# A convolution half-chunk moved behind the first half's sums, and the last output chunk finished by 128 tokens

## The chip, the cores and the metric

The kernel runs on one core of a Trainium2 chip, all work in one launch. The metric is the device time of one execution in microseconds (us). Before the change the median of three runs is 1165.35 us (1165.35 to 1165.51).

A core has five instruction streams that meet only at semaphores: TensorE (PE, matmuls; PEld is its weight load, which runs beside them), VectorE (DVE), ScalarE (ACT), GpSimd (POOL) and SyncE (SP, which here only issues DMAs). Each stream runs its instructions in the order in which the program wrote them.

## The reference, cut to what matters

Two layers over 512 tokens of width 1024, in float32. Layer 0 mixes by gating and attention, layer 1 by a convolution module; each is followed by a squared-ReLU MLP. The two places that the change touches are the convolution of layer 1 and the last norm.

```python
def conformer_conv(h, w_pw1, b_pw1, w_dw, b_dw, ln_g, ln_b, w_pw2, b_pw2):
    a, gate = jnp.split(h @ w_pw1 + b_pw1, 2, axis=-1)
    y = a * jax.nn.sigmoid(gate)
    y = lax.conv_general_dilated(y, w_dw[:, None, :], ...)   # 31 taps along the tokens, each channel alone
    y = jax.nn.silu(layernorm(y, ln_g, ln_b))                # over the 1024 channels of a token
    return y @ w_pw2 + b_pw2
...
x = x + g2 * sq_relu_mlp(...)
return rmsnorm(x, final_g)
```

## The kernel before

**Layout.** Everything is transposed: channels lie on the 128 partitions in 8 chunks, tokens along the free axis (512, in two halves of 256, a0:a1 and b0:b1). Each float32 product is made of three matmuls from a high and a low part (`mm3`, line 87; `together`, line 214, does it for several output chunks at once). The order on every engine is the order in which the Python code is run; no scheduler moves anything (`manual_schedule`).

**The convolution module** (`conv_module`, from line 1360). `glu(c)` makes channel chunk c of the gated input, for c = 2 to 7 here (0 and 1 were made in the norm before). Chunks 1 and 2 are convolved on DVE, tap by tap, from a queue of small jobs (`aux`, `work`). Chunks 0, 3, 4, 5, 6, 7 are convolved on PE: `evac_glu` copies the padded chunk into four tiles `y4` of 32 channels at four shifts (16 copies of 32 partitions, lines 1307 to 1314), all by DMA on SP, but of chunk 7 ten by DMA and six by ACT (line 1312). `conv_steps` (line 1327) then makes 32 matmuls for a half of 256 tokens, one after another into one PSUM bank, and ACT adds the bias (line 1336) into `zc`. It is a generator that can stop between steps of k.

**The layer norm over channels** needs, for each token, the sum and the sum of squares over all 8 chunks. `take(c)` (line 1345) subtracts a base value (line 1349), squares on ACT (line 1356) and adds to the two running sums (lines 1357, 1358). When the last chunk of a half is in, `sums` (line 1418) adds over the partitions by eight tiny matmuls (line 1422) and makes mean and variance (lines 1424 to 1426), and POOL the inverse root (line 1427); `stats` n = 0 and 1 spread mean and inverse root over the partitions by two matmuls each (line 1434), and ACT copies them to `mur` (line 1436). `normed` is a generator over chunks: subtract (1444), scale (1447), SiLU (1452), split in high and low part (lines 93, 94). Its outputs `ch` are the operands of the next product, `together(four, ch, ...)`, whose first matmul therefore waits for chunk 0 of `normed`.

**The order around the change.** Written a for the first half of the tokens and b for the second, PE does 5a, 5b, 6a, 7a, 6b, `sums` of half a, a first piece of 7b, `stats` 0, a second piece, `stats` 1, the rest of 7b, then the product. `W.pieces(4)` between 5b and 6a cuts the four pieces of a weight tile in high and low parts (line 148 on ACT, line 143 on DVE) and, with the last, has the next tile loaded on SP (line 124).

**The end** (`tail1`). Output chunk 7 of half b is the last product. Before the change, DVE adds it to `x` in one instruction of 256 tokens (line 1073), ACT squares it (line 343), and PE sums the squares over the partitions by two matmuls for each 128 tokens (line 1575): one over `acc` (chunks 0 to 6), one over the last square. Then root (1577), reciprocal (1578), spread by PE (1581), copy (1583), eight multiplications (1586) and four output DMAs on SP (1588).

In the trace one matmul of float32 operands shows as two records, so a half chunk of 32 matmuls has 64.

Of the kernel before, what the change touches and what calls it, by code (L numbers as in the profile page):

```python
# [13 lines left out]
AF = mybir.ActivationFunctionType  # L14
# [3 lines left out]
P = 128  # L18
# [4 lines left out]
H = T // 2  # L23
# [32 lines left out]
def body(ctx: ExitStack, tc: tile.TileContext, I: dict, out: bass.AP):  # L56
    nc = tc.nc
    act, dve, pool, pe, sync = nc.scalar, nc.vector, nc.gpsimd, nc.tensor, nc.sync
# [19 lines left out]
    def slot(dt=F32, cols=512, s="t"):  # L78
        return bp.tile([P, cols], dt, tag="tmp", name=nm(s), bufs=6)
# [92 lines left out]
    for l in range(2):  # L172
        s = [I["w_ff1"][l, i] for i in range(4)]
        for g in range(1, 4):
# [5 lines left out]
    W = Weights([w_in[i] for i in (4, 5, 8, 9, 6, 7, 2, 3, 0, 1)] + [I["w_out"][i] for i in range(4)]  # L180
                + ff_srcs[0] + [I["w_pw1"][i] for i in range(8)] + [I["w_pw2"][i] for i in range(4)]
                + ff_srcs[1])
# [31 lines left out]
    def together(ms, acts, evac, t0=0, t1=T, ks=range(KC), hook=None):  # L214

        ks = list(ks)
        pss = [bank()[:, : t1 - t0] for _ in ms]
        for n, k in enumerate(ks):
            a = acts[k][0][:, t0:t1], acts[k][1][:, t0:t1]
            for (m, w, c), ps in zip(ms, pss):  # L220
                pe.matmul(ps, w[0][:, k, c : c + P], a[0], start=n == 0, stop=False)  # L221
                pe.matmul(ps, w[1][:, k, c : c + P], a[0], start=False, stop=False)  # L222
            for (m, w, c), ps in zip(ms, pss):
                pe.matmul(ps, w[0][:, k, c : c + P], a[1], start=False, stop=n == len(ks) - 1)  # L224
            if hook:
                hook(n)
        return [lambda m=m, ps=ps: evac(m, ps, t0, t1) for (m, w, c), ps in zip(ms, pss)]
# [31 lines left out]
    for k in range(0, KC, 2):  # L259
        t = mpa.tile([P, 2, 512], F32, tag="ablk", name=nm("x0"), bufs=6)  # L260
# [42 lines left out]
    for k in range(0, KC, 4):  # L303
        t = mpa.tile([P, 4, TC], F32, tag="ablk", name=nm("ctx"), bufs=6)
# [4 lines left out]
    ones = cp.tile([P, P], F32, name="ones")  # L309
# [108 lines left out]
    for k in range(KC):  # L418
        sq = slot(s="sq")
# [649 lines left out]
        sync.dma_start(x[:, 4 * i : 4 * i + 4, :], I["xT"][:, 4 * i : 4 * i + 4, :])  # L1069

    def residual(gate, ss):
        def evac(m, ps, t0, t1):
            dve.scalar_tensor_tensor(x[:, m, t0:t1], ps, gate[:, m : m + 1], x[:, m, t0:t1],  # L1073
                                     op0=ALU.mult, op1=ALU.add)
            if ss is not None:
                ss.add(x[:, m, t0:t1], t0, t1)
        return evac

# [248 lines left out]
    def conv_steps(c, t0, t1, stops=()):  # L1327
        wd = cv["matrices"][c]
        ps = bank()[:, : t1 - t0]
        for k in range(8):  # L1330
            if k in stops:
                yield
            for g in range(4):
                pe.matmul(ps[32 * g : 32 * g + 32, :], wd[:, g * 8 + k, :],  # L1334
                          cv["y4"][c, g][:, 4 * k + t0 : 4 * k + t1], start=k == 0, stop=k == 7)
        act.activation(zs[c][:, t0:t1], ps, AF.Identity, bias=vcol(V_BDW, c))
        yield

    def conv_pe(c, t0=0, t1=T):
        run(conv_steps(c, t0, t1))  # L1340
# [4 lines left out]
    def take(c, t0=0, t1=T):  # L1345

        lsum, lsq = cv["sums"]
        z = zs[c][:, t0:t1]
        dve.tensor_tensor(z, z, cv["m0"][:, t0:t1], op=ALU.subtract)
        if not cv["begun"]:  # L1350
            cv["begun"] = True
            dve.tensor_copy(lsum[:, t0:t1], z)
            act.activation(lsq[:, t0:t1], z, AF.Square)
        else:
            sq = slot(cols=t1 - t0, s="sq")
            act.activation(sq, z, AF.Square)
            dve.tensor_tensor(lsum[:, t0:t1], lsum[:, t0:t1], z, op=ALU.add)
            dve.tensor_tensor(lsq[:, t0:t1], lsq[:, t0:t1], sq, op=ALU.add)

    def conv_module(h):  # L1360
# [46 lines left out]
        preload(AF.Silu)  # L1407
        work(100)
        conv_pe(5, a0, a1)
        conv_pe(5, b0, b1)  # L1410
        take(5)
        W.pieces(4)
        conv_pe(6, a0, a1)
        lsum, lsq = cv["sums"]
        ch = [pair(s="ch") for _ in range(KC)]
        stat = {}

        def sums(t0, t1):
            ps = bank()[:, :4]
            for i in range(4):  # L1420
                b = t0 + i % 2 * P
                pe.matmul(ps[:, i : i + 1], (lsum, lsq)[i // 2][:, b : b + P], ones[:, :1], start=True, stop=True)  # L1422
            q = small(8, "q")
            dve.tensor_scalar(q[:, 0:4], ps, 1.0 / D, None, op0=ALU.mult)
            dve.tensor_tensor(q[:, 4:6], q[:, 0:2], q[:, 0:2], op=ALU.mult)
            dve.scalar_tensor_tensor(q[:, 4:6], q[:, 2:4], EPS, q[:, 4:6], op0=ALU.add, op1=ALU.subtract)
            pool.tensor_tensor(q[:, 2:4], q[:, 4:6], expo[:, :2], op=ALU.pow)
            stat[t0] = q, vp.tile([P, T], F32, tag="mur", name=nm("mur"), bufs=2), bank()

        def stats(t0, n):  # L1430

            q, r, ps = stat[t0]
            for i in (2 * n, 2 * n + 1):
                pe.matmul(ps[:, i * P : (i + 1) * P], q[:, i : i + 1].to_broadcast([P, P]), ident,  # L1434
                          start=True, stop=True)
            act.copy(r[:, n * H : n * H + H], ps[:, n * H : n * H + H])
# [18 lines left out]
        def go(gen, n=1):  # L1455
            for _ in range(n):
                next(gen, None)
# [2 lines left out]
        conv_pe(7, a0, a1)  # L1460
        take(7, a0, a1)
        conv_pe(6, b0, b1)
        sums(a0, a1)
        last = conv_steps(7, b0, b1, (1, 4))
        next(last)
        stats(a0, 0)
        na = normed(a0, a1)
        take(6, b0, b1)
        go(na)
        next(last)  # L1470
        stats(a0, 1)
        go(na, 2)
        next(last)
        go(na)
# [57 lines left out]
    def tail1(acts, ev, ss, ff, third):  # L1532

        (a0, a1), (b0, b1) = HALVES
        oa, ob = (wp.tile([P, KC, H], F32, tag="raw", name=nm("o"), bufs=2) for _ in range(2))

        def gained(ks, o=ob, t0=b0, t1=b1):
            for k in ks:
                act.activation(o[:, k, :], x[:, k, t0:t1], AF.Copy, scale=vcol(V_FG, k))

        def finish(ks, r):
            for k in ks:
                dve.scalar_tensor_tensor(oa[:, k, :], x[:, k, a0:a1], vcol(V_FG, k), r, op0=ALU.mult, op1=ALU.mult)  # L1543
            sync.dma_start(out[:, ks[0] : ks[-1] + 1, a0:a1], oa[:, ks[0] : ks[-1] + 1, :])

        w = W.use()
        for i in range(2):
            chunk(4 + i, w, i * P, acts, ev, 0, t0=a0, t1=a1)
        v = W.use()
        for i in range(2):  # L1550
            chunk(6 + i, v, i * P, acts, ev, 0, t0=a0, t1=a1)
            gained((2 * i, 2 * i + 1))
        gained((6, 7), oa, a0, a1)
        four = together([(4, w, 0)], acts, ev, b0, b1, hook=lambda n: ss.total(a0, a1) if n == 5 else None)[0]
        four()
        r = ss.rstd(a0, a1)
        finish((0, 1, 2), r)
        gained((4,))
        chunk(5, w, P, acts, ev, 0, t0=b0, t1=b1)
        finish((3, 4, 5), r)  # L1560
        gained((5,))
        chunk(6, v, 0, acts, ev, 0, t0=b0, t1=b1)
        for k in (6, 7):
            pool.tensor_tensor(oa[:, k, :], oa[:, k, :], r, op=ALU.mult)
        sync.dma_start(out[:, 6:8, a0:a1], oa[:, 6:8, :])
        gained((6,))
        ss.flush()
        seven = together([(7, v, P)], acts, ev, b0, b1)[0]
        seven()
        gained((7,))  # L1570
        sq, ss.late = ss.late[0], None
        tot_ = bank()
        for n in range(2):
            for i, t in enumerate((ss.acc[:, b0:b1], sq)):
                pe.matmul(tot_[:, n : n + 1], t[:, n * P : n * P + P], ones[:, :1], start=i == 0, stop=i == 1)
        q = small(2, "q")
        act.activation(q, tot_[:, :2], AF.Sqrt, bias=epsc, scale=1.0 / D)
        dve.reciprocal(q, q)
        pr = bank()[:, :H]
        for n in range(2):  # L1580
            pe.matmul(pr[:, n * P : n * P + P], q[:, n : n + 1].to_broadcast([P, P]), ident, start=True, stop=True)
        r = slot(cols=H, s="rstd")
        act.copy(r, pr)
        for e, ks in ((dve, (0, 1)), (pool, (2,)), (dve, (3, 4)), (pool, (5,)), (dve, (6, 7))):
            for k in ks:
                e.tensor_tensor(ob[:, k, :], ob[:, k, :], pr if e is dve else r, op=ALU.mult)
        for k0, k1 in ((0, 1), (1, 3), (3, 6), (6, 8)):
            sync.dma_start(out[:, k0:k1, b0:b1], ob[:, k0:k1, :])
        ff.close()

    mlp(1, lead1, 0, tail1)
# [84 lines left out]
```

## Time and profile before

| | |
|---|---|
| median of three runs | 1165.35 us |
| the profiled execution: its own time, its span | 1164.55 us, 1162.8 us |
| ACT and POOL, share of the span busy | 41%, 13% |
| DMA traffic, mean over the span | 139 GB/s |
| longest idle time of PE by the profile's list of waits | 1.0 us, at the start |

A page of the profile has times from one execution on the chip; a line of a timeline gives start, duration, engine, line of the program, operation, output and inputs, how many instructions were merged, and in brackets the idle time ahead of it with what ended it. Matmul records overlap: a record of 256 columns lasts 0.28 to 0.4 us while the next one starts 0.12 us later, so stretches are read from starts, not from durations. A stretch of merged matmuls counts as busy also where it contains a short wait.

### The profile page before, as it was taken

The page shows a single profiled execution, that of the slowest core. Times are in us where ns is not written, and L with a number is a line of the kernel's source. Part 1 is how long each engine was busy: PE and PEld are TensorE (multiplying, and loading weights), DVE is VectorE, ACT ScalarE, POOL GpSimd, SP SyncE. Part 2 cuts the span into 40 slices and gives each one's busy share as a digit, 9 for nine tenths or more (in the row PEclk, how much of TensorE's full clock was granted, in tenths as well). Part 3 has the DMA queues.
Part 4 walks back from the last instruction along what each step waited for, and adds up shares of the span by engine and source line. Part 5 has one row for each costly group of instructions (what it writes and reads, how often), then busy time and mean ns, then how long its engine had stood idle before and what let it go on. Part 6 is the DMA issues. An engine that isn't in the chain of part 4 may idle for free. (4 is left out here: it accounts for less than half of the span.)

```text
span 1162.8 us, 16541 instructions
## 1 busy us (share of the span) xinstructions
PE 1150.3 (99%) x6612; PEld 956.9 (82%) x6612; DVE 724.8 (62%) x1258; ACT 479.7 (41%) x955; POOL 153.0 (13%) x149
## 2 busy tenths in 40 slices
PE   9999999999999999999999999999999999999997
PEld 5788898889888888888889666699888888888887
DVE  4855786878665665666677879577643443443544
ACT  5564557446422422423246223575531331332423
POOL 0041234433000000000024110153100000000001
PEclk9999999999999999999999999999999999999998
DMA  9634543351565555555531444313232232232222
GB/s 370 247 125 134 167 149 110 121 192 62 205 236 181 188 210 181 191 207 181 203 123 56 145 126 125 98 37 110 73 109 100 82 109 102 79 109 78 105 73 73
DMA packets 32333, 161.91 MB, mean 139 GB/s; under 512 B 4416, under 2 KB 8000, under 8 KB 16256
## 3 DMA queue, kind: packets, MB, share of 16 engines
q1 hardware_dynamic: 28224, 146.43, 36.5%
q10 hardware_dynamic: 4032, 14.42, 3.6%
q8 instruction: 52, 0.85, 0.3%
q14 instruction: 25, 0.20, 0.1%
HBM read 152.52 MB, written 2.10 MB: 133 GB/s over the span
## 5 line engine op out<-in xcount | busy, mean ns | idle before, releaser
L148 ACT CAST whi<-raw 128x512 fp32r<-128x512 f32 x340 | 191.5, 616 | 196.4 <-PE ps L90 171.9
L88 PE MATMUL ps<-hhi,whi 128*128 128x512 f32 x608 | 238.5, 392 | 0.0
L89 PE MATMUL ps<-hhi,wlo 128*128 128x512 f32 x608 | 236.8, 389 | 0.0
L90 PE MATMUL ps<-hlo,whi 128*128 128x512 f32 x608 | 236.8, 389 | 0.0
L143 DVE TENSOR_TENSOR wlo<-raw,whi 128x512 fp32r<-128x512 f32 x293 | 200.3, 721 | 37.1 <-ACT whi L148 36.3
L90 PE MATMUL ps<-hid,whi 128*128 128x512 f32 (+1 forms) x520 | 196.5, 378 | 0.0
L89 PE MATMUL ps<-hid,wlo 128*128 128x512 f32 (+1 forms) x520 | 196.5, 378 | 0.0
L88 PE MATMUL ps<-hid,whi 128*128 128x512 f32 (+1 forms) x520 | 196.4, 378 | 0.0
L1073 DVE SCALAR_TENSOR_TENSOR x<-ps,mod,x 128x512 f32<-128x512 f32 (+1 forms) x94 | 62.7, 669 | 147.5 <-PE ps L90 142.6
L88 PEld LDWEIGHTS ps<-hhi,whi 128*128 128x128 f32 x608 | 114.2, 188 | 26.6 <-issue 3.2
L90 PEld LDWEIGHTS ps<-hlo,whi 128*128 128x128 f32 x608 | 114.1, 188 | 23.9
L89 PEld LDWEIGHTS ps<-hhi,wlo 128*128 128x128 f32 x608 | 114.2, 188 | 23.0
L143 POOL TENSOR_TENSOR wlo<-raw,whi 128x512 fp32r<-128x512 f32 x47 | 70.0, 1503 | 416.9 <-DVE mod L599 306.8
L599 DVE CUSTOM_DVE_ANT_0 graw<-graw,cB,vec 128x1024 f32<-128x1024 f32 x80 | 109.0, 1364 | 20.8 <-DMA graw<-in_wmB_dram 20.8
L89 PEld LDWEIGHTS ps<-hid,wlo 128*128 128x128 f32 x520 | 97.9, 188 | 18.2
L88 PEld LDWEIGHTS ps<-hid,whi 128*128 128x128 f32 x520 | 97.8, 188 | 18.2
L90 PEld LDWEIGHTS ps<-hid,whi 128*128 128x128 f32 x520 | 97.9, 188 | 17.9
L1209 DVE TENSOR_TENSOR z<-z 128x512 f32<-128x512 f32 (+1 forms) x72 | 46.8, 656 | 90.8 <-ACT z L1207 90.7
L1207 ACT ACTIVATE z<-ps 128x512 f32<-128x512 f32 (+1 forms) x72 | 38.9, 549 | 131.5 <-PE ps L90 129.3
L1213 DVE TENSOR_TENSOR hid<-z,hid 128x512 fp32r<-128x512 f32 (+1 forms) x72 | 45.7, 641 | 43.3 <-ACT hid L1211 43.3
L1211 ACT CAST hid<-z 128x512 fp32r<-128x512 f32 (+1 forms) x72 | 40.6, 572 | 60.6 <-DVE z L1209 60.6
L343 ACT ACTIVATE sq<-x 128x256 f32<-128x256 f32 (+1 forms) x41 | 20.3, 496 | 66.4 <-DVE x L1073 66.3
(271 smaller groups left out, 1712.3 us busy)
## 6 DMA issues: line engine op xcount, KB each, us to landing
raw<-in_w_ff_dram SPq DMA_DIRECT2D x64, 1024.0 KB
graw<-in_wmB_dram SPq DMA_DIRECT2D x28, 1024.0 KB
graw<-in_wmB_dram ACTq DMA_DIRECT2D x24, 512.0 KB
raw<-in_w_pw_dram SPq DMA_DIRECT2D x12, 1024.0 KB
raw<-in_w_in_dram SPq DMA_DIRECT2D x8, 1024.0 KB
wmA<-in_wmA_dram SPq DMA_DIRECT2D x7, 1024.0 KB
y<-ypad SPq DMA_DIRECT2D x90, 67.5 KB
raw<-in_w_out_dram SPq DMA_DIRECT2D x4, 1024.0 KB
```

The lines of the kernel that those rows point to most:

```text
L88: pe.matmul(ps, w[0], a[0], start=first, stop=False)
L89: pe.matmul(ps, w[1], a[0], start=False, stop=False)
L90: pe.matmul(ps, w[0], a[1], start=False, stop=last)
L143: (e or dve).tensor_tensor(lo.parts[q], src, hi.parts[q].bitcast(F32), op=ALU.subtract)
L148: act.copy(hi.parts[q], src)
L343: act.activation(sq, src, AF.Square)
L599: dve.tensor_tensor_reduce(out=wv, in0=wv, in1=cB, scale=1.0, scalar=vcol(V_BMOD, l * 48 + q * 8 + j % 8), op0=ALU.mult, op1=ALU.add, accu ...
L1073: dve.scalar_tensor_tensor(x[:, m, t0:t1], ps, gate[:, m : m + 1], x[:, m, t0:t1], op0=ALU.mult, op1=ALU.add)
L1207: act.activation(z, ps, AF.Relu)
L1209: dve.tensor_tensor(z, z, z, op=ALU.mult)
L1211: act.copy(hi, z)
L1213: dve.tensor_tensor(lo, z, hi.bitcast(F32), op=ALU.subtract)
```

## The change

In the convolution, chunk 5 is convolved for half a only at first. Its half b is done as `five`, behind `sums` of half a, in two pieces around `stats` 0, and 7b is done in two pieces behind `stats` 1. The four weight pieces, which stood together, are spread: behind 5a, 6a, 6b and 5b. `take(5)` is split into its halves; `take(5, b0, b1)` comes last but one. At the end, the residual add and the square of the last chunk are done for 128 tokens at a time, the two matmuls over `acc` come first, and the matmul over a square follows each square. The third of the four last output DMAs is issued by ACT.

```diff
     def residual(gate, ss):
-        def evac(m, ps, t0, t1):
+        def evac(m, ps, t0, t1, sq=None):
             dve.scalar_tensor_tensor(x[:, m, t0:t1], ps, gate[:, m : m + 1], x[:, m, t0:t1], ...)
-            if ss is not None:
+            if sq is not None:
+                act.activation(sq, x[:, m, t0:t1], AF.Square)
+            elif ss is not None:
                 ss.add(x[:, m, t0:t1], t0, t1)
...
         conv_pe(5, a0, a1)
-        conv_pe(5, b0, b1)
-        take(5)
-        W.pieces(4)
+        W.pieces(1)
+        take(5, a0, a1)
         conv_pe(6, a0, a1)
+        W.pieces(1)
...
         conv_pe(7, a0, a1)
         take(7, a0, a1)
         conv_pe(6, b0, b1)
+        W.pieces(1)
         sums(a0, a1)
-        last = conv_steps(7, b0, b1, (1, 4))
-        next(last)
+        five, last = conv_steps(5, b0, b1, (4,)), conv_steps(7, b0, b1, (4,))
+        next(five)
+        take(6, b0, b1)
         stats(a0, 0)
         na = normed(a0, a1)
-        take(6, b0, b1)
         go(na)
+        next(five)
+        W.pieces(1)
+        stats(a0, 1)
         next(last)
-        stats(a0, 1)
+        take(5, b0, b1)
         go(na, 2)
         next(last)
...
-        seven = together([(7, v, P)], acts, ev, b0, b1)[0]
-        seven()
-        gained((7,))
-        sq, ss.late = ss.late[0], None
+        last = []
+        together([(7, v, P)], acts, lambda m, ps, t0, t1: last.append(ps), b0, b1)[0]()
+        sq = slot(cols=H, s="sq")
         tot_ = bank()
         for n in range(2):
-            for i, t in enumerate((ss.acc[:, b0:b1], sq)):
-                pe.matmul(tot_[:, n : n + 1], t[:, n * P : n * P + P], ones[:, :1], start=i == 0, stop=i == 1)
+            pe.matmul(tot_[:, n : n + 1], ss.acc[:, b0 + n * P : b0 + n * P + P], ones[:, :1],
+                      start=n == 0, stop=False, skip_group_check=True)
+        for n in range(2):
+            t = slice(n * P, n * P + P)
+            ev(7, last[0][:, t], b0 + n * P, b0 + n * P + P, sq[:, t])
+            pe.matmul(tot_[:, n : n + 1], sq[:, t], ones[:, :1], start=False, stop=True, skip_group_check=True)
+        gained((7,))
...
-            sync.dma_start(out[:, k0:k1, b0:b1], ob[:, k0:k1, :])
+            (act if k0 == 3 else sync).dma_start(out[:, k0:k1, b0:b1], ob[:, k0:k1, :])
```

How the instructions stand now, at three places. First PE, where its second half-chunk of this stretch ends. The names y_923 to y_926 are the four tiles of chunk 5, y_937 to y_940 those of chunk 6, y_952 to y_955 those of chunk 7; in brackets stand the semaphores that a row waits for, those of DMAs by queue. Before:

```order
3703 L1334 MATMUL ps_6615<-y_925_6320,graw_5871 32x256
3704 L1334 MATMUL ps_6615<-y_926_6325,graw_5871 32x256
3705 L1334 MATMUL ps_6666<-y_937_6421,graw_5871 32x256 [waits DMAHW3_49,DMAHW2_49,DMAHW4_49,DMAHW1_49,Pool_49]
3706 L1334 MATMUL ps_6666<-y_938_6426,graw_5871 32x256 [waits DMAHW6_49,DMAHW7_49,DMAHW5_49,DMAHW0_49]
3707 L1334 MATMUL ps_6666<-y_939_6431,graw_5871 32x256 [waits DMAHW3_49,DMAHW4_49,DMAHW2_49,DMAHW1_49]
3708 L1334 MATMUL ps_6666<-y_940_6436,graw_5871 32x256 [waits DMAHW6_49,DMAHW7_49,DMAHW5_49,DMAHW0_49]
```

And with the change, in the same rows:

```order
3703 L1336 MATMUL ps_6624<-y_939_6431,graw_5871 32x256
3704 L1336 MATMUL ps_6624<-y_940_6436,graw_5871 32x256
3705 L1336 MATMUL ps_6681<-y_952_6559,cB 32x256 [waits DMAHW4_49,DMAHW5_49,DMAHW3_49,DMAHW2_49]
3706 L1336 MATMUL ps_6681<-y_953_6564,cB 32x256 [waits DMAHW6_49,DMAHW7_49,DMAHW1_49,DMAHW0_49]
3707 L1336 MATMUL ps_6681<-y_954_6569,cB 32x256 [waits DMAHW3_49,DMAHW2_49,Activation_49]
3708 L1336 MATMUL ps_6681<-y_955_6574,cB 32x256 [waits Activation_49]
```

Chunk 7 stood third among the half-chunks behind the last `glu` product (5a, 5b, 6a came first) and now stands one half-chunk, 32 matmuls, earlier.

Second ACT, from the bias of 6b (zc_6420) to the first operand of the product (chhi). zc_6309 is chunk 5, zc_6558 chunk 7, zc_5834 chunk 0. Before:

```order
567 L1336 ACTIVATE zc_6420<-ps_6760,vec 128x256 [waits PE_49]
568 L1436 COPY mur_6804<-ps_6805 128x256 [waits PE_49]
569 L1356 ACTIVATE sq_6815<-zc_6420 128x256 [waits DVE_49]
570 L1436 COPY mur_6804<-ps_6805 128x256 [waits DVE_49,PE_49]
571 L1452 ACTIVATE zc_5834<-zc_5834,vec 128x256 [waits DVE_49]
572 L93 CAST chhi_6700<-zc_5834 128x256 [waits Activation_49]
```

With the change:

```order
566 L1338 ACTIVATE zc_6420<-ps_6720,vec 128x256 [waits PE_49]
567 L148 CAST whi_6615<-raw_6408 128x512
568 L1358 ACTIVATE sq_6786<-zc_6420 128x256 [waits DVE_49,Activation_49]
569 L1438 COPY mur_6766<-ps_6767 128x256 [waits PE_49]
570 L1338 ACTIVATE zc_6309<-ps_6768,vec 128x256 [waits PE_49]
571 L148 CAST whi_6615<-raw_6408 128x512
572 L1438 COPY mur_6766<-ps_6767 128x256 [waits DVE_49,PE_49]
573 L1358 ACTIVATE sq_6836<-zc_6309 128x256 [waits DVE_49,Activation_49]
574 L1454 ACTIVATE zc_5834<-zc_5834,vec 128x256 [waits DVE_49]
575 L93 CAST chhi_6660<-zc_5834 128x256 [waits Activation_49]
```

Four instructions came in: two weight casts, and the bias and the square of 5b. On DVE the matching low parts (line 143) and the three instructions of `take(5, b0, b1)` came in ahead of the scaling of chunk 0 (line 1447).

Third PE at the end of the program, from the last matmul of the last product on. Before:

```order
5914 L224 MATMUL ps_9982<-hid_9535,whi_9768 128x256
5915 L1575 MATMUL ps_10011<-ones,acc_9637 128x1 [waits DVE_49]
5916 L1575 MATMUL ps_10011<-ones,sq_10008 128x1 [waits Activation_49]
5917 L1575 MATMUL ps_10011<-ones,acc_9637 128x1
5918 L1575 MATMUL ps_10011<-ones,sq_10008 128x1
```

With the change:

```order
5914 L224 MATMUL ps_9987<-hid_9540,whi_9773 128x256
5915 L1579 MATMUL ps_10013<-ones,acc_9642 128x1 [waits DVE_49]
5916 L1579 MATMUL ps_10013<-ones,acc_9642 128x1
5917 L1584 MATMUL ps_10013<-ones,sq_10012 128x1 [waits Activation_49] x2
5918 L1591 MATMUL ps_10026<-kon,q_10023 128x128 [waits DVE_49]
```

Both matmuls over `acc` now stand ahead of the first that waits for a square.

## The prediction

> **What bounds the kernel now.** The page first: the share of each engine, and the clock by slices.
>
> ```profile
> span 1162.8 us, 16541 instructions
> PE 1150.3 (99%) x6612; PEld 956.9 (82%) x6612; DVE 724.8 (62%) x1258; ACT 479.7 (41%) x955; POOL 153.0 (13%) x149
> ...
> PEclk9999999999999999999999999999999999999998
> ```
>
> PE is the bound, at its full clock to the last slice. So a change of order can only win PE's idle time or shorten the end, and loses what it adds of either. Next the timeline of PE over the convolution, to find the idle time there.
>
> ```profile
> 725.38 10.57 PE L1334 MATMUL ps<-y,graw 128*32 128x256 f32 x192
> 735.77 0.59 PE L1334 MATMUL ps<-y,cB 128*32 128x256 f32 x2
> 736.55 4.14 PE L1334 MATMUL ps<-y,cB 128*32 128x256 f32 x60 [0.19 <-issue]
> ...
> 744.29 1.05 PE L1422 MATMUL ps<-ones,lsum 128*128 128x1 f32 x8
> ...
> 745.85 0.71 PE L1434 MATMUL ps<-kon,q 128*128 128x128 f32 x4
> 746.49 1.50 PE L1334 MATMUL ps<-y,cB 128*32 128x256 f32 x24
> 748.53 0.68 PE L1434 MATMUL ps<-kon,q 128*128 128x128 f32 x4 [0.54 <-DVE zc L1444]
> 749.14 1.94 PE L1334 MATMUL ps<-y,cB 128*32 128x256 f32 x32
> 751.20 0.39 PE L221 MATMUL ps<-chhi,whi 128*128 128x256 f32 x1
> ```
>
> The reader sees 5a, 5b and 6a as one block: 192 records in 10.57 us, so 3.52 us for each half chunk and 0.055 us a record. Then 7a (the rows with cB) limps until about 737.2; then it and 6b run dense; `sums` at 744.29; 7b in pieces with 0.54 us of idle time in front of `stats` 1; the product begins at 751.20. The idle time that can be won is that 0.54 us, the limping of 7a, and a few tenths. PEld shows 7a better:
>
> ```profile
> 736.52 0.14 PEld L1334 LDWEIGHTS ps<-y,cB 128*32 128x32 f32 x2 [0.64 <-issue]
> 737.23 2.98 PEld L1334 LDWEIGHTS ps<-y,cB 128*32 128x32 f32 x58 [0.57 <-ACT zc L1336]
> ```
>
> The first tile of chunk 7 is there when PE comes, the second at 736.52, the third at 737.23. The profile names an ACT bias for the last, but the tile hangs on two DMAs and two ACT copies, so I look at SP.
>
> ```profile
> 721.56 3.12 SPq L1314 DMA_DIRECT2D y<-ypad  x5
> 726.51 0.33 SPq L124 DMA_DIRECT2D raw<-in_w_pw_dram  x1
> ...
> L1314 SPq DMA_DIRECT2D y<-ypad x10: 507/585/1799, 727.2 to 733.9; - x10
> ...
> 726.00:726.50 0.50, 0.50 (x18) 0.27 (x10) 0.50 (x2) 0.00 (x0) 0.00 (x0) 1.00 0.00 0
> ```
>
> The ten DMAs of chunk 7 are issued from 727.2 to 733.9, behind a weight load that shares the DMA engines. The five issues before them end at 724.68; one takes 0.585 us, so the last began at about 724.1, and by 726.0 the DMA engines are idle (last row, 0.00): 2.0 us from issue to landing. The last of chunk 7 began at 733.9 and should land at 735.9; PE got it at 737.23. It is **a transfer, not PE, that sets when 7a runs**.
>
> **The change part by part.** *5b out of the way of 7a.* PE now reaches 7a after two half chunks, at 725.38 + 2 x 3.52 = 732.42, and nothing in SP's order or in the weight load ahead moves. So PE waits where it used to work. Until when? At the latest 737.23, as now. At the earliest 735.9, without what delayed that last DMA by 1.3 us; it is an estimate from these rows:
>
> ```profile
> q8 instruction: 52, 0.85, 0.3%
> ...
> q8 instruction: 1, 0.02, 4.4%
> ```
>
> The first is of the whole span, the other of 733.5 to 735.5: one packet of instructions is fetched in the midst of the copies, and the issue beside it took 1.799 us. 6612 matmuls on 52 packets are 127 on one: the pace of PE's own stream. In this run it came at some 154 records behind 725.38 (8.5 us by 0.055); the new order has only 128 records ahead of 7a, so the same fetch falls behind the copies. I take 735.9, a gain of 1.33 us on the start of 7a, and keep 0 as the other end. PE's wait grows from about 1.3 us to 3.5, with one pair of records at each landed tile.
>
> *From 7a to the product.* Behind the start of 7a everything is as before up to `sums`; from there to the product it was 751.20 - 744.29 = 6.91 us. Now (clock at 0 with `sums`): 1.0 for it, first part of 5b 1.76, `stats` 0 0.7, second part 1.76: 5.25. The bias of 5b on ACT comes next, then a chain across engines:
>
> ```profile
> 744.40 0.47 ACT L1336 ACTIVATE zc<-ps,vec 128x256 f32<-128x256 f32 x1 [2.07 <-PE ps L1334]
> 734.66 2.16 ACT L148 CAST whi<-raw 128x512 fp32r<-128x512 f32 x4
> 735.39 2.49 DVE L143 TENSOR_TENSOR wlo<-raw,whi 128x512 fp32r<-128x512 f32 x4
> 745.85 0.42 DVE L1349 TENSOR_TENSOR zc<-zc,m 128x256 f32<-128x256 f32 x1
> 749.65 0.42 DVE L1447 TENSOR_TENSOR zc<-zc,ps 128x256 f32<-128x256 f32 x1 [1.27 <-ACT mur L1436]
> 750.11 0.60 ACT L1452 ACTIVATE zc<-zc,vec 128x256 f32<-128x256 f32 x1 [0.49 <-DVE zc L1447]
> 750.74 0.40 ACT L93 CAST chhi<-zc 128x256 fp32r<-128x256 f32 x1
> ```
>
> Bias of 5b from 5.6 (6b's began at 744.40, 0.11 us behind the next PE work, and that is here `stats` 1 at 5.45) to 6.1; weight cast 0.54 to 6.6; low part on DVE 0.62 to 7.3; `take(5)` three instructions of 0.42 with the square between, to 8.6; scale of chunk 0 0.42 to 9.0; SiLU and cast 1.05 with hand-overs of about 0.05, to 10.1. So the product begins at 10.1 instead of 6.91: **+3.2 us**. PE's own work comes to 9.7 (5.25, `stats` 1 0.7, 7b 3.52, change-overs 0.2), so the bounds are +2.8 and +3.2; I take 3.2, the later of the two. What had hidden 5b before was the wait for the transfer; now it stands uncovered, and of the stalls it was to fill only 0.54 us and some tenths go. The product's own waits stay as they are, and the later weight load (line 124, behind the fourth piece) lands 20 us ahead of its use: nothing.
>
> Sum for the convolution: 3.2 - 1.33 = **+1.9** (bounds 1.5 and 3.2).
>
> *The end.* The chain before:
>
> ```profile
> 1152.72 0.28 PE L224 MATMUL ps<-hid,whi 128*128 128x256 f32 x1
> 1153.04 0.48 DVE L1073 SCALAR_TENSOR_TENSOR x<-ps,mod,x 128x256 f32<-128x256 f32 x1
> 1153.61 0.42 ACT L343 ACTIVATE sq<-x 128x256 f32<-128x256 f32 x1 [0.63 <-DVE x L1073]
> 1153.93 0.49 ACT L1539 ACTIVATE o<-x,vec 128x256 f32<-128x256 f32 x1
> 1154.08 0.38 PE L1575 MATMUL ps<-ones,sq 128*128 128x1 f32 x2 [0.60 <-ACT sq L343]
> ...
> 1154.55 0.36 PE L1575 MATMUL ps<-ones,sq 128*128 128x1 f32 x2
> 1154.95 0.26 ACT L1577 ACTIVATE q<-ps,epsc 128x2 f32<-128x2 f32 x1 [0.52 <-PE ps L1575]
> 1129.59 0.75 DVE L1073 SCALAR_TENSOR_TENSOR x<-ps,mod,x 128x512 f32<-128x512 f32 x1 [2.19 <-PE ps L90]
> 1130.37 0.63 ACT L343 ACTIVATE sq<-x 128x512 f32<-128x512 f32 x1 [3.77 <-DVE x L1073]
> ```
>
> By 512 and 256 tokens, 128 cost 0.35 us on DVE and 0.31 on ACT. Add 1 ends at 1153.39, add 2 at 1153.65, squares at 1153.79 and 1154.05, the last pair of records runs 1154.10 to 1154.46, and the root starts at 1154.50 instead of 1154.95, with the copy of line 1539 (0.49 us, on ACT ahead of it) just out of the way. **-0.45 us**, bounds 0 and -0.6. The DMA on ACT: nothing, because the third issue waits for POOL and the fourth for DVE either way, and behind the first landing the output runs at the DMA engines' rate.
>
> *The clock.* Nothing in the trace shows PE waiting 3.5 us amid dense work. Its nearest rows are the end, where dense work stops with the matmul of 1152.72 and only scattered records follow, and the start:
>
> ```profile
> 1153.00:1156.30 3.30, 1.92 (x12) 1.56 (x12) 0.68 (x3) 1.11 (x4) 0.00 (x0) 1.00 0.47 160
> 1156.40:1158.00 1.60, 0.00 (x0) 0.00 (x0) 1.33 (x4) 0.24 (x1) 1.23 (x2) 0.50 0.01 4
> L406 PE MATMUL ps<-ones x6: 894/1062/1222, 1.0 to 5.4; 128*128 128x512 f32 x6
> L406 PE MATMUL ps<-ones x5: 592/592/894, 5.4 to 7.4; 128*128 128x512 f32 x5
> ```
>
> At the end the granted clock fell from 1.00 to 0.50 at 1156.3, 3.3 us after dense work, with twelve records in between. At the start the same matmul lasts 1.06 us up to about 6.0 and 0.59 after: half speed for 5.0 us of unbroken work, then full. So the new wait may cost the clock, and 7a and 6b would then start at 1.2 GHz: between nothing and half of 5.0, 2.5 us. I take the middle, **+1.25**: the wait is as long as the stretch at the end, and as poor in matmuls.
>
> The Trainium skill, page "TensorE: Matmul & The Clock Gate", section "HAM oscillation — how this bites in real kernels", tells of a kernel whose bursts of matmuls each start cold because a wait for a DMA in between throttled the array. By that rule the clock term is certain, without it the term is 0. The trace agrees as far as the fall at the end goes; no run here shows a fall in front of a burst.
>
> Total: 1.9 - 0.45 + 1.25 = +2.7. The profiled execution took 1164.55 us in itself (span 1162.8), the median of three is 1165.35; the difference goes on the median: **1168.0 us**, +0.23%.
>
> **The rivals.** *The clock holds* during the wait (as it did at 735.8 to 737.2): 1165.35 + 1.9 - 0.45 = 1166.8, not slower by more than 0.2% (2.3 us, about what a measurement of this kernel can tell from no change). For it: the 1.3 us wait of today left 1.00. *The fetch still falls among the copies*, or something else delays the last one: 7a starts at 737.2, the wait is 4.8 us, 1168.1 without and 1169.4 with the clock term. *The copies are there in time*, because they land sooner than SP's rows make me think: at 734.5 the conv's loss and the end's gain cancel (3.2 - 0.45 = 2.75 before 737.23); with no wait at 732.42 the time would be 1163.3, faster by under 0.2%. Against it: the last issue begins only at 733.9. *The end does nothing*, because the second half's hand-overs eat the gain: 0.45 more on any case.
>
> **How the numbers follow.** Forecast (wait and half clock) 0.45, clock holds 0.31, fetch still in the way 0.13, copies in time 0.05, the end for nothing 0.06. The range goes from 1166.3, clock held with a shorter chain, to 1169.6, late copies with the clock term. Faster needs the copies in time and more, 0.04; same is the clock held and the lower edge of the forecast, 0.44; slower the rest, 0.52.
>
> **What would show it.** In the profile after: 5a and 6a end near 732.4, then two lone pairs, then dense matmuls with cB from 735.9 (737.2 if the fetch is in the way); the clock of the stretch behind is 0.50 or 1.00, and half chunks take 7.0 or 3.5 us; `sums` to first product 10 us; the root 0.45 us earlier behind the last L224. I am wrong if 7a follows 6a at once, or if the stretch from 725.4 to the product takes under 26 us (25.8 before).

## The result and the profile after

The changed kernel takes 1168.61 us (median of 8 runs, 1166.94 to 1170.31), the kernel before 1165.43 us in the same session: a ratio of 1.0026, with a 95% interval of 1.0017 to 1.0036. So it is slower, by about 3.2 us. The profiled execution of the changed kernel took 1169.09 us, with a span of 1167.3 us. The page after, its first rows and the clock by slices:

```profile
span 1167.3 us, 16549 instructions
PE 1151.8 (99%) x6612; PEld 957.4 (82%) x6612; DVE 729.6 (63%) x1262; ACT 480.1 (41%) x957; POOL 152.0 (13%) x149
...
PEclk9999999999999999999999999999999999999998
```

PE has as many instructions as before and is busy 1.5 us longer, though it has no more to compute. That is already a hint of a slower clock, but the slices of 29 us show no dip; it has to be looked for in short windows. The timeline of PE over the convolution of the changed kernel, with PEld's row of the third tile (start, duration, line, operation, count, and in brackets the idle time ahead with what ended it):

```profile
726.30 7.11 PE L1336 MATMUL ps<-y,graw 128*32 128x256 f32 x128
735.15 0.59 PE L1336 MATMUL ps<-y,cB 128*32 128x256 f32 x2 [1.73 <-DMA y<-ypad]
736.13 0.59 PE L1336 MATMUL ps<-y,cB 128*32 128x256 f32 x2 [0.39 <-DMA y<-ypad]
737.48 0.72 PEld L1336 LDWEIGHTS ps<-y,cB 128*32 128x32 f32 x16 [1.24 <-ACT whi L148]
737.51 5.12 PE L1336 MATMUL ps<-y,cB 128*32 128x256 f32 x58 [0.79 <-DMA y<-ypad]
...
746.23 1.05 PE L1424 MATMUL ps<-ones,lsum 128*128 128x1 f32 x8
747.21 1.93 PE L1336 MATMUL ps<-y,graw 128*32 128x256 f32 x32
749.07 0.71 PE L1436 MATMUL ps<-kon,q 128*128 128x128 f32 x4
749.71 1.93 PE L1336 MATMUL ps<-y,graw 128*32 128x256 f32 x32
...
752.22 3.66 PE L1336 MATMUL ps<-y,cB 128*32 128x256 f32 x64
756.18 0.39 PE L221 MATMUL ps<-chhi,whi 128*128 128x256 f32 x1 [0.30 <-ACT chhi L93]
```

Read from the top: 5a and 6a are one block of 128 records up to about 733.3; then 7a should follow, the third half chunk of this stretch now and the fourth before, but there are only two lone pairs of records until chunk 7's third tile comes at 737.48 (PEld's row names an ACT cast there, PE's the DMA, which is the last to come); 5b stands in two pieces of 32 records, one on each side of `stats` 0; 7b stands whole; and the product waits 0.30 us for ACT. From 5a to the product it is 756.18 - 726.30 = 29.88 us, where it was 751.20 - 725.38 = 25.82. The 58 records of 7a last 5.12 us where a whole half chunk should last 3.5. The windows of that stretch show why (busy time and count of each engine, granted clock, DMA share, GB/s):

```profile
733.30:737.50 4.20, 1.30 (x8) 0.30 (x5) 2.54 (x6) 2.40 (x7) 0.00 (x0) 1.00 0.33 80
737.50:738.00 0.50, 0.49 (x10) 0.38 (x14) 0.47 (x3) 0.10 (x1) 0.00 (x0) 0.94 0.00 0
738.00:741.30 3.30, 3.30 (x36) 2.10 (x32) 0.75 (x2) 0.32 (x1) 0.00 (x0) 0.50 0.02 5
741.40:742.50 1.10, 1.10 (x28) 0.81 (x24) 0.00 (x0) 0.00 (x0) 0.00 (x0) 1.00 0.00 0
```

While PE waits (eight records in 4.20 us) the granted clock is still 1.00. In this execution it falls just after the dense work has begun again, stays at 0.50, the 1.2 GHz level, and comes back at about 741.35. In the slow window 36 records take 3.30 us, 0.092 us each, where it is 0.055 in the dense blocks.

The end of the changed kernel, in the timeline:

```profile
1157.70 0.28 PE L224 MATMUL ps<-hid,whi 128*128 128x256 f32 x1
...
1158.46 0.51 ACT L1076 ACTIVATE sq<-x 128x128 f32<-128x128 f32 x2 [0.50 <-DVE x L1073]
1158.82 0.61 PE L1584 MATMUL ps<-ones,sq 128*128 128x1 f32 x4
...
1159.46 0.26 ACT L1587 ACTIVATE q<-ps,epsc 128x2 f32<-128x2 f32 x1
```

From the last L224 to the root it is 1159.46 - 1157.70 = 1.76 us, where it was 1154.95 - 1152.72 = 2.23.

The difference of the two spans, 1167.3 - 1162.8 = 4.5 us, divides like this:

| part | before, us | after, us | difference |
|---|---|---|---|
| start of the span to 5a, ahead of all that was changed | 725.38 | 726.30 | +0.92 |
| 5a to chunk 7's third tile (PEld) | 11.85 | 11.18 | -0.67 |
| third tile to `sums` | 7.06 | 8.75 | +1.69 |
| `sums` to the product | 6.91 | 9.95 | +3.04 |
| last L224 to the end of the span | 10.08 | 9.60 | -0.48 |

The rows make the whole 4.5, so the stretch between the product and the last L224 is as long as before. The first lies ahead of every moved instruction: 5a starts between 725.4 and 726.7 in all the executions profiled here, that of a kernel with the old convolution too (725.93). Without it the parts make +3.6 us, against the +3.2 of the medians.

### The profile page after: what moved, and what is told of

Its sections match the earlier page's. It is cut to its first block, busy times and chain, and to the rows that moved or that the text cites. A ratio compares the mean times of both kernels' runs of the same rounds, so it can differ in the third digit from the quotient of the medians.

```text
span 1167.3 us, 16549 instructions
## 1 busy us (share of the span) xinstructions
PE 1151.8 (99%) x6612; PEld 957.4 (82%) x6612; DVE 729.6 (63%) x1262; ACT 480.1 (41%) x957; POOL 152.0 (13%) x149
## 4 chain that ended last, share of the span: by engine, by line
PE 88%; DVE 5%; ACT 3%; DMA 3%; issue 1%; SPq 0%; DVEq 0%; ACTq 0%
PE ps L88 22%; PE ps L89 22%; PE ps L90 22%; PE ps L224 3%; PE ps L221 3%; PE ps L222 3%; PE ps L1336 3%; PE ps L493 2%; DMA graw<-in_wmB_dram 2%; ACT s L926 1%; PE ps L955 1%; DVE graw L599 1%; PE ps L909 1%; PE ps L457 1%; PE ps L939 1%
## 5 line engine op out<-in xcount | busy, mean ns | idle before, releaser
L1073 DVE SCALAR_TENSOR_TENSOR x<-ps,mod,x 128x512 f32<-128x512 f32 (+2 forms) x95 | 62.8, 664 | 147.3 <-PE ps L90 142.5
```

## The experiments

Each ratio is against the kernel before, run on the same chip in the same session, with its 95% interval. That kernel took 1165.43 us in the session of the result and 1165.89 and 1165.75 in the other two, so kernels of different sessions are compared by their distance from it.

**The end alone.** The old convolution with the new end, that is, these edits without the moved 5b:

```diff
+        def evac(m, ps, t0, t1, sq=None):
+            if sq is not None:
+                act.activation(sq, x[:, m, t0:t1], AF.Square)
...
+        for n in range(2):
+            t = slice(n * P, n * P + P)
+            ev(7, last[0][:, t], b0 + n * P, b0 + n * P + P, sq[:, t])
+            pe.matmul(tot_[:, n : n + 1], sq[:, t], ones[:, :1], start=False, stop=True, skip_group_check=True)
```

> The old convolution with the new end (128-token add and square, sums reordered, third output DMA on ACT). Theory: the end alone gives 0.47 us, so 1164.9 to 1165.0 against 1165.4 before (ratio 0.9996); in the profile 1.76 us from the last L224 to the root instead of 2.23, and 9.6 us from there to the end of the span instead of 10.1. Rival: the gain at the root is lost again at the output DMAs, whose rate then sets the end: 10.1 us to the end, time as before.

Measured: 1165.45 us (11 runs) against 1165.89, ratio 0.9994 (0.9985 to 1.0003). The size is the one forecast, -0.44 us, though the interval includes no change. The end of its profiled execution:

```profile
1152.99 0.28 PE L224 MATMUL ps<-hid,whi 128*128 128x256 f32 x1
...
1154.76 0.26 ACT L1583 ACTIVATE q<-ps,epsc 128x2 f32<-128x2 f32 x1
...
1155.27 1.15 PE L1587 MATMUL ps<-kon,q 128*128 128x128 f32 x4 [0.55 <-DVE q L1584]
```

The root comes 1.77 us behind the last L224, as in the changed kernel. Behind it the four spreading matmuls took 1.15 us here: the granted clock averaged 0.53 from 1155.3 to 1156.3. In the changed kernel the same four take 0.71. The end of the span came 10.0 us behind the last L224 (1163.0 - 1152.99), not the expected 9.6 and hardly less than the 10.08 before. So a clock that falls a little sooner can eat most of this gain in single executions.

**The convolution alone.** The new order of the convolution with the old end, all edits at the end taken back.

> The new convolution order with the old end. Theory: the changed kernel plus 0.47 us, 1169.1 (ratio 1.0031), with third tile 11.2 us after the start of 5a, a fall of the clock to 0.50 around 7a for 3.4 us in most executions, sums to product 9.9 us. Rival: the two parts act on one another (end and convolution not additive): a difference of over 1 us from that.

Measured: 1169.23 us (9 runs), ratio 1.0025 (1.0015 to 1.0034). PE's timeline of its profiled execution:

```profile
726.29 7.11 PE L1334 MATMUL ps<-y,graw 128*32 128x256 f32 x128
...
736.76 4.87 PE L1334 MATMUL ps<-y,cB 128*32 128x256 f32 x58 [0.80 <-DMA y<-ypad]
...
745.23 1.05 PE L1422 MATMUL ps<-ones,lsum 128*128 128x1 f32 x8
...
755.18 0.39 PE L221 MATMUL ps<-chhi,whi 128*128 128x256 f32 x1 [0.30 <-ACT chhi L93]
```

All of the loss is here: 28.89 us from 5a to the product. The 58 records last 4.87 us, so the clock falls here as well, but at another point. The windows of the wait and of the records behind it:

```profile
736.30:736.70 0.40, 0.00 (x0) 0.00 (x0) 0.08 (x1) 0.40 (x1) 0.00 (x0) 0.50 0.00 0
736.80:739.70 2.90, 2.90 (x28) 1.50 (x32) 1.88 (x4) 0.42 (x1) 0.00 (x0) 0.50 0.02 6
```

The clock is at 0.50 while PE still waits, and the burst begins slow. From `sums` to the product it is 9.95 again. The third tile comes 10.47 us after 5a, the very 10.5 that the prediction had worked out (735.9 - 725.38); in the changed kernel's profile it came at 11.18. This kernel is 3.5 us over the kernel before and the whole change 3.2, which leaves -0.3 us for the end, beside the -0.47 of the rows.

**Filling the wait.** To see what the fall of the clock costs, PE is given matmuls of `ones` between 6a and 7a, whose result nobody uses:

```diff
+        idle = bank()
+        for _ in range(8):
+            pe.matmul(idle, ones, ones.unsqueeze(1).to_broadcast([P, 4, P]), start=True, stop=True)
         conv_pe(7, a0, a1)
```

> The changed kernel with eight matmuls of constants (512 columns, 3.4 us in all, result unused) between 6a and 7a, where PE waits for chunk 7's copies. Theory: the wait is set by the copies, so the filling costs nothing, and it saves what the fall of the clock took: 7a dense in 3.3 us instead of 5.0, granted clock 1.00 throughout the convolution, 1.7 us less than the changed kernel, +1.4 us on the kernel before (ratio 1.0012). Rival 1: the clock's fall costs nothing that counts (another chain sets the start of the product): as the changed kernel, 1.0026. Rival 2: the filling itself delays 7a: +3.4 us more.

Measured: 1170.74 us (5 runs), ratio 1.0038 (1.0026 to 1.0051): 4.8 us over the kernel before, not 1.4. PE's timeline shows the reason:

```profile
733.55 7.13 PE L1464 MATMUL ps<-ones 128*128 128x512 f32 x16
740.61 3.66 PE L1336 MATMUL ps<-y,cB 128*32 128x256 f32 x64
```

Each of these matmuls is two records, and eight of them last 7.1 us, twice what I had meant to fill. 7a is held up to 740.61, 14.1 us after 5a, when its tiles are long there. That 7a then lasts 3.66 us says that the clock held, but the kernel measures the filling. So again with four:

```diff
-        for _ in range(8):
+        for _ in range(4):
```

> The changed kernel with four matmuls of constants between 6a and 7a (the run with eight showed 0.44 us for each record and two records for each matmul, so 3.5 us now, 10.6 us after the start of 5a, ahead of the third tile at 11.2). Theory: the filling fits into the wait, the clock stays at 1.00 through 7a, 7a takes 3.3 us instead of 5.0: 1.7 us less than the changed kernel where that one falls, so about 1167 (+1.4 us, ratio 1.0012). Rival: the wait's price is not the clock; then as the changed kernel, 1168.6.

Measured: 1167.47 us (11 runs, 1166.73 to 1168.24), ratio 1.0014 (1.0006 to 1.0023). The windows of the filling and of 7a, then PE's timeline:

```profile
733.70:737.30 3.60, 3.60 (x12) 1.44 (x8) 1.98 (x5) 2.36 (x6) 0.00 (x0) 1.00 0.35 85
737.30:740.80 3.50, 3.50 (x65) 2.11 (x68) 1.77 (x4) 0.42 (x1) 0.00 (x0) 1.00 0.02 5
```

```profile
726.66 7.11 PE L1336 MATMUL ps<-y,graw 128*32 128x256 f32 x128
733.70 3.70 PE L1464 MATMUL ps<-ones 128*128 128x512 f32 x8
737.33 3.66 PE L1336 MATMUL ps<-y,cB 128*32 128x256 f32 x64
...
744.38 1.05 PE L1424 MATMUL ps<-ones,lsum 128*128 128x1 f32 x8
```

Now 7a begins 10.67 us after 5a without a pause and runs at 1.00 throughout: 7.05 us to `sums` where the changed kernel needed 8.75. Useless work makes the kernel about 1.5 us faster than the change (1.7 us over the kernel before instead of 3.2). The clock is not all of that: in this execution 7a also begins 0.51 us sooner after 5a than in the changed kernel's (10.67 instead of 11.18), since its copies were earlier. What is left over the kernel before, 1.7 us, is what the clock does not explain.

The runs of the changed kernel point the same way. Its eight times, each beside the mean granted clock of the whole span:

| time, us | 1166.94 | 1167.53 | 1167.93 | 1168.48 | 1168.74 | 1169.09 | 1169.67 | 1170.31 |
|---|---|---|---|---|---|---|---|---|
| clock | .998 | .998 | .996 | .996 | .996 | .996 | .995 | .996 |

The two at .998 are the fastest; they average 1167.24 us and the other six 1169.04. The difference of 1.8 us is about the 1.7 us that 7a lost in the profile. All runs with four filling matmuls have .997 or .998. Still, this mean does not tell where in the span the clock fell: the kernel before has runs from .996 to .998 too. That 7a kept its clock in those two runs is likely, not shown.

**The weight load behind the copies.** Ahead of the ten DMAs of chunk 7 SP issues a weight load, and before it issues the eighth of them it waits until that load has landed. The profile's list of SP's waits from 726 to 736 shows it, first in the kernel before, then in the changed kernel (who waited, for what, us in total, times, longest):

```profile
SPq L1314 <- DMA raw<-in_w_pw_dram: 0.8, 1, 0.8
SPq L1316 <- DMA raw<-in_w_pw_dram: 1.0, 1, 1.0
```

Here the load is held back until the copies are out, so SP does not wait for it, and it does not share the DMA engines with them:

```diff
-                    self.load()
+                    if not self.held:
+                        self.load()
...
+        W.held = True
         glu(7)
+        W.held = False
+        W.load()
```

> The changed kernel with the weight load that stands ahead of chunk 7's copies on SP issued behind them. Theory: the copies are late because SP issues them one by one at 0.6 us and two of them wait for or share with that load; without it the last is issued 5.6 us after the first and lands 2.0 us later, so 7a's third tile comes about 9.5 us after the start of 5a instead of 11.2: 1.7 us less than the changed kernel, and up to 1.7 more if the clock then holds (1165.2 to 1167). Rival: the load has no part in it: as the changed kernel, 1168.6.

Measured: 1166.41 us (10 runs), ratio 1.0006 (0.9997 to 1.0015). PE's timeline:

```profile
725.94 7.11 PE L1338 MATMUL ps<-y,graw 128*32 128x256 f32 x128
732.87 0.59 PE L1338 MATMUL ps<-y,cB 128*32 128x256 f32 x2
734.55 0.62 PE L1338 MATMUL ps<-y,cB 128*32 128x256 f32 x2 [1.09 <-DMA y<-ypad]
735.88 3.43 PE L1338 MATMUL ps<-y,cB 128*32 128x256 f32 x58 [0.70 <-DMA y<-ypad]
```

SP's wait for the load is gone, and its last copy is issued at 733.7, 7.8 us after 5a instead of 9.0. The first tile is there when 6a ends, and the third 9.94 us after 5a instead of 11.18, in both kernels 2.2 us behind the last issue. PE's wait is shorter, and in this execution the clock held (58 records in 3.43 us). The two effects make 2.95 us of the profile (29.88 - 26.93 from 5a to the product) and 2.7 of the medians: most of what the change had lost, for one load issued later. Of the ten runs the two slowest, 1167.90 and 1168.02, have a mean clock of .996 and the others, up to 1166.82, .997 or .998; so it may have fallen in these two.

**No transfer at all.** If the transfer sets 7a, it should follow 6a at once when other engines make the copies. Of chunk 7's sixteen copies SP's DMAs made ten and ACT six; now DVE makes eight, POOL two and ACT six:

```diff
-                    if c == 7 and 4 * g + u > 9:
-                        act.copy(to, of)
+                    if c == 7:
+                        n = 4 * g + u
+                        (act.copy if n > 9 else pool.tensor_copy if n % 4 == 3 else dve.tensor_copy)(to, of)
```

> The changed kernel with chunk 7's sixteen shifted copies made by DVE (8), POOL (2) and ACT (6), none by DMA, so that they are done by about 6 us after the last glu product. Theory: the wait for the transfer and the clock's fall are the whole reason for the loss, so 7a follows 6a at once (7.1 us after the start of 5a instead of 11.2), the clock stays at 1.00, sums to product stays at 9.9 us: 1165.4 - (11.85 - 7.1) + 3.0 - 0.47 = 1163.2 (ratio 0.998). Rival: the longer way from sums to product (3.0 us) and work added to DVE ahead of it are the loss: 1166 or more.

Measured: 1162.93 us (6 runs, 1162.23 to 1163.45), ratio 0.9972 (0.9961 to 0.9984): the fastest kernel of this study. PE's timeline:

```profile
726.37 7.11 PE L1337 MATMUL ps<-y,graw 128*32 128x256 f32 x128
733.30 3.64 PE L1337 MATMUL ps<-y,cB 128*32 128x256 f32 x64
...
740.33 1.05 PE L1425 MATMUL ps<-ones,lsum 128*128 128x1 f32 x8
...
750.28 0.39 PE L221 MATMUL ps<-chhi,whi 128*128 128x256 f32 x1 [0.30 <-ACT chhi L93]
```

7a begins 6.93 us after 5a, without a gap, and from 5a to `sums` PE is dense: 13.96 us, four half chunks. `sums` to product stays 9.95. That is 23.91 us from 5a to the product, 5.97 less than the changed kernel; the medians, 3.0 under the kernel before and 3.2 over it, differ by 6.1.

**The quick copies under the old order.** Is it the copies alone that win, or the new order with them? The same copies, the new end, but 5b back in front of 7a:

> The old convolution order with chunk 7's copies made by the engines (as in the quick variant of the new order), and the new end. Theory: 7a follows 6a at once, 10.6 us after the start of 5a instead of 11.85, sums to product stays 6.9 us with its 0.5 us of idle time ahead of the second spread: 1.3 + 0.47 = 1.8 us under the kernel before, 1163.7 (ratio 0.9985), and some 0.7 us over the quick variant of the new order, since only there the idle time of the old order is filled. Rival: the new order gives nothing even when the copies are in time; then this one is as fast as the quick new one, 1162.9, or faster.

Measured: 1163.57 us (11 runs), ratio 0.9981 (0.9973 to 0.9990). Its timeline of PE:

```profile
726.46 10.57 PE L1337 MATMUL ps<-y,graw 128*32 128x256 f32 x192
...
748.10 0.68 PE L1437 MATMUL ps<-kon,q 128*128 128x128 f32 x4 [0.54 <-DVE zc L1447]
...
750.77 0.39 PE L221 MATMUL ps<-chhi,whi 128*128 128x256 f32 x1
```

From 5a to the product it is 24.31 us, and the 0.54 us of idle time ahead of `stats` 1 is back. With early tiles the new order is worth 24.31 - 23.91 = 0.4 us by the rows; by the medians it is 0.8 (3.0 and 2.2 under the kernel before), with intervals that overlap. So most of the gain is the copies', and the new order adds a little on top of them.

**One weight piece out of the chain.** In the chain from `sums` to the product stands the fourth piece of weights, a cast on ACT. With the quick copies, it is moved behind the second part of the norm:

```diff
         next(five)
-        W.pieces(1)
...
         go(na, 2)
+        W.pieces(1)
```

> The quick variant of the new order with the fourth weight piece (a cast on ACT, the low part on DVE) moved from behind 5b to behind the first steps of the norm. Theory: that piece stands in the chain from 5b's bias to the first operand, which sets the product's start by a little over PE's own work: sums to product 9.7 us instead of 9.95, 0.25 us less in the profile, within the noise of the times. Rival: the chain was not what PE waited for: 9.95 as before, or the piece now delays a later operand of the product.

Measured: 1163.18 us (9 runs), ratio 0.9975 (0.9965 to 0.9985), not to be told from the 0.9972 without the edit. Its `sums` start at 740.64, and the row of the product has no wait any more:

```profile
750.23 0.39 PE L221 MATMUL ps<-chhi,whi 128*128 128x256 f32 x1
```

That is 9.59 us instead of 9.95: the chain is no longer behind PE, and PE's own work is the rest. The 0.36 us do not show in the times; with intervals of some 2 us they could not.

## Why the prediction was right

The forecast was 1168.0 us in a range of 1166.3 to 1169.6; 1168.61 was measured, slower, by the main mechanism: 5b stands uncovered, and PE waits for a transfer where 5b was. The size of two terms was off. The steps, in their order:

**A transfer sets 7a, and PE waits where 5b was.** Shown. In the changed kernel PE waits for a DMA ahead of each of chunk 7's first three tiles, and only earlier tiles change that: without the transfers 7a follows 6a at once, with the load behind them the third tile comes 1.24 us sooner.

**7a begins 1.33 us earlier.** The mechanism was there, the size was half: 0.67 us in the changed kernel's profile. The row of SP's issues in the changed kernel (count, shortest, median and longest in ns, first and last start), and from its DMA queues between 735.5 and 739 the instruction packet:

```profile
L1316 SPq DMA_DIRECT2D y<-ypad x10: 507/585/1243, 728.1 to 735.3; - x10
```

```profile
q8 instruction: 1, 0.02, 1.6%
```

The packet has moved behind the copies' issues, as forecast, and the last tile is there 2.2 us after the last issue begins (737.48 - 735.3, with PEld's start), where it took 3.3 before (737.23 - 733.9) and I had taken 2.0. The size failed at the start of that issue: 9.0 us after 5a instead of 8.5. The prediction let nothing move in the weight load ahead of the copies, but SP issues the last three copies only when that load has landed, and here it waited 1.0 us for it instead of 0.8. The long issue of 1.243 us does not count, since it lies ahead of that wait. With the same ten DMAs in the same order the kernel with the convolution alone waited 0.6 us, issued the last at 8.3 and had its tile at 10.47. So the gain was 0.67 and 1.4 us in these two executions, and the 1.33 lay near the better one. Why the load lands sooner in one execution than in another stays open; with the load behind the copies, the tile came at 9.94.

**From `sums` to the product 10.1 us instead of 6.91.** Right: 9.95, and within 0.01 of that in every profile that has this order with that piece of weights in place. The chain ran by the rows that the prediction named. In the timeline of the changed kernel, on ACT and DVE, in order of time:

```profile
751.72 0.47 ACT L1338 ACTIVATE zc<-ps,vec 128x256 f32<-128x256 f32 x1 [1.52 <-PE ps L1336]
752.09 0.61 ACT L148 CAST whi<-raw 128x512 fp32r<-128x512 f32 x1
...
754.30 0.42 DVE L1360 TENSOR_TENSOR lsum<-lsum,sq 128x256 f32<-128x256 f32 x1
755.09 0.60 ACT L1454 ACTIVATE zc<-zc,vec 128x256 f32<-128x256 f32 x1 [0.82 <-DVE zc L1449]
755.72 0.40 ACT L93 CAST chhi<-zc 128x256 fp32r<-128x256 f32 x1
```

With 0 at `sums` (746.23): the bias of 5b begins at 5.49 (5.6 in the prediction), the last of the `take` ends at 8.49 (8.6), the cast ends at 9.89 (10.1). Of the +3.04 about 2.7 is PE's (9.59 - 6.91, by the run without the weight piece in the chain): 5b's 3.52, which had been hidden in the wait for the transfer, less the idle time that it fills now. The other 0.36 is the chain behind it.

**The end, -0.45.** Right: -0.47 from the last L224 to the root, and -0.48 to the end of the span. The copy on ACT did not get in the way, and no effect of the output's DMA on ACT shows: from the root to the end of the span it is 7.84 us (1167.3 - 1159.46) and was 7.85.

**The clock, +1.25, taken from the middle of 0 to 2.5.** It fell in the profile and, as far as the mean clock tells, in six of the eight runs, and cost 1.7 us: it stayed low for about 3.4 us, not for the 5.0 from which the upper bound came. So the term was 0.45 too small for an execution in which it falls. The outcome is about 0 or about 1.7, not the middle, and that the middle suits the median of a mixture of both is in part luck. The rival in which the clock holds was real: two runs, at 1166.94 and 1167.53, a little above the 1166.8 worked out for it. In the profiles here the clock held behind the shorter wait of the kernel with the late weight load (third tile 9.94 us after 5a) and fell at the longer ones of the changed kernel (11.18) and of the convolution alone (10.47).

The rule of the Trainium skill that the prediction weighed ("TensorE: Matmul & The Clock Gate", "HAM oscillation — how this bites in real kernels", bursts that start cold after a wait for a DMA) now has rows in front of a burst. The kernel with the convolution alone agrees with it: the clock was at 0.50 from 736.30, and its burst began cold at 736.76. In the changed kernel the burst began warm at 737.51 and turned cold in its first half microsecond, and by the mean clock of the runs the fall was not certain, as by that rule alone it would have been.

**The sum.** Worked out again with what was measured, 3.04 - 0.67 + 1.7 - 0.48 = +3.6 us for the profiled execution, and +3.2 for the medians, where +2.7 was forecast. The two terms that were off, 0.66 too much gain for 7a and 0.45 too little for the clock, point the same way and make the missing microsecond in the profile.

## What to carry to other kernels

Work that seems to stand in front of a wait for a transfer can be its cover: moved away, it costs its time where it lands (here about 2.7 of 3.52 us), and the wait that opens is worth only as much as the transfer really comes sooner. So first ask what sets the late operand; here the same copies, made by engines that had time instead of by small DMAs, took about 6 us off the changed kernel, more than its order had cost. Ask also what the late transfer itself waits for: the copies stood behind a weight load on the same queue, and issuing that load after them won most of the loss back. And a wait of a few microseconds in front of dense matmuls can have a second price, the clock of the stretch behind it, which no idle row shows.

## What the runs showed of the hardware

- Around PE's wait for the copies the granted clock fell from 1.00 to 0.50 and stayed there for about 3.4 us, but not at a fixed point. In the changed kernel it was 1.00 up to 737.50, through the wait, and fell after the dense work had begun again; in the kernel with the convolution alone it was 0.50 from 736.30 to 736.70, while PE still waited. It seems not to fall in every execution of the same program: two of eight had a mean of .998, the others .995 or .996.
- Filling the wait with unused matmuls kept the clock at 1.00 through 7a, and with four of them the kernel was 1.5 us faster than with the empty wait, part of it by earlier copies. A float32 matmul of 512 columns took 0.89 us (eight in 7.13), so a filling is easily made too long: with eight the kernel lost 1.7 us to the change instead.
- Ten small copies from SBUF to SBUF, issued in the same order, were through 9.9 to 11.9 us after 5a. With a weight load ahead of them SP held the eighth issue for 0.5 to 1.6 us, depending on the execution, until that load had landed; without it there was no such wait. Before the change an instruction packet came beside the last issue, which then took 1.799 us instead of 0.585. Sixteen copies spread over DVE, POOL and ACT were through by 6.93 us in both profiles with the new order, with no wait on PE.
